# A causal convolution of 31 taps by 128 odd frequencies of 256 points with a transform of 60 points for its wrapped sums, and weight splits in another order around it

## Chip, core and metric

One core of a Trainium2 chip runs the whole kernel in one launch. The metric is the device time in microseconds (us); a run's time is that of one execution, and the profile is of one further execution on the same kind of chip.

## What is computed

One decoder layer for 256 tokens of width 1024, in float32: RMS norm, one input projection, eight heads of causal attention beside a convolution branch, an output projection over both with a residual, then a gated feed-forward network (width 2816) with a residual. The branch that the change is about, cut from the reference:

```
h = a * sigmoid(g)                      # (256 tokens, 512 channels)
h = pad(h, 30 tokens in front)          # causal
h = depthwise_conv(h, dw_w, 31 taps) + dw_b
h = silu(layer_norm(h over channels))   # becomes the lower half of the output projection's input
x = x + concat([attn, h]) @ w_out
```

## The kernel before

**Precision by splitting.** Every float32 operand of TensorE is split into a high part (a rounded copy, by ScalarE) and a low part (the difference, by VectorE), both of type float32r; a product is two or three matmuls (hi·hi, hi·lo, lo·hi). So each weight costs ScalarE one copy (`wh`, L196) and VectorE one subtraction (`wl`, L200) for every piece of 128 x 1024.

**Order of the work.** TensorE's program is written out by hand. Tasks (generators) are put between its groups of matmuls: `step()` runs what is due, `spawn` adds one. Every engine runs its instructions in the order in which they were written. Weights come in 47 blocks of 1 MB on SyncE's queue into four buffers. `feed(upto)` writes the copies `wh` up to piece upto+1 and the subtractions `wl` up to piece upto, and behind each odd `wl` the load of a block four further on. Seven piece buffers are in turn.

**The convolution.** It is done by frequencies, as matrix products with constant cosine and sine tables. `conv_task` makes `hf` (L230 and the two lines before it, by `mm3`): the transform over 288 points, which holds the 256 tokens and the 30 wrapped ones, has 145 frequencies. Real and imaginary parts of the first 128 fill two tiles of 128 rows (j = 0, 1), the 17 others with copies fill 68 rows of a third (j = 2). Each needs both token blocks of 128: 3 tiles x 2 blocks x 3 matmuls of 512 columns. VectorE multiplies by the taps' spectrum `Ws` (L546 to L548, L553) into `Y`; Y's rows are split into `yh`, `yl` (L181, L182). `ln_task` transforms back: two token blocks x 3 tiles x 3 matmuls into two PSUM banks `cv`; the third tile has a row of ones times `dw_b`, which adds the bias. Then come the statistics of the layer norm (`st`, `mv`, L578, L579), a reciprocal root by twelve small VectorE operations (L240 to L257) that ends in `nb` (L583), the normalised copy `yn` (L588, ScalarE), the transpose `cT` (L599, TensorE), Silu into `cs` (L602) and the split into `mix` (L181, L182).

**Around it.** The tile j = 2 is not made in the task: `third()` runs after the last group of the input projection (`p`, L624), between the two copies of the values `vs` (L631, L632, both ScalarE) and the attention's last products `O` (L644, L645). Behind `O` come the 18 matmuls of `cv`, and behind them the output projection in two halves of 8 groups of 12 matmuls `po` (L236): the first half takes the attention's rows of `w_out`, the second the convolution's. Each group ends in an addition on VectorE, `x2T` (L686), which frees the group's PSUM bank; there are four such banks in turn, shared with `p`, `O` and the feed-forward's `fg` and `fu`. In the second half, two ScalarE operations (`g` high L660, square `sq` L662), one on GpSimd (`acc`, L664) and one on VectorE (`g` low, L667) follow each `x2T`: they make the input of the feed-forward network and its sum of squares (`pss`, L698, then a root, `wide`, L703, and a transpose `prb`, L707).

In the input projection `feed` stops at piece 21. At each group of the output projection it is called with the piece of the group plus LEAD = 4, less one for the last two groups of the second half; a piece serves two groups. So the first group (piece 20) has the low parts of pieces 22, 23 and 24 written ahead of its `x2T`.

Of the kernel before, what the change touches and what calls it, by code (L numbers as in the profile page):

```python
# [9 lines left out]
F32R = mybir.dt.float32r  # L10
I32 = mybir.dt.int32
BF16 = mybir.dt.bfloat16
AF = mybir.ActivationFunctionType
ALU = mybir.AluOpType
AX = mybir.AxisListType

P = 128
D = 1024
T = 256
# [6 lines left out]
NF = FF // P  # L26
TAPS = 31
EPS = 1e-6
L = 288
NB = 47  # L30
BW = 2048
PIECE = 1024
R3 = 69
WARM = 18
RAW = 4
WGT = 7
# [31 lines left out]
def _parts(a):  # L68

    hi = _round12(a)  # L70
    return np.stack([hi, a - hi], 1)


def _constants():
    t = np.arange(T)[:, None]
    f = np.arange(L // 2 + 1)[None, :]
    ang = 2 * np.pi * ((t * f) % L) / L
    c, s = np.cos(ang), np.sin(ang)
    alpha = np.where((f == 0) | (f == L // 2), 1.0, 2.0) / L
    fwd = np.concatenate([c[:, :P], -s[:, :P], c[:, P:], -s[:, P:], c[:, P:], -s[:, P:]], 1)  # L80
    fwd = _parts(fwd.astype(np.float32).reshape(NT, P, 324).transpose(1, 0, 2))
    ir, ii = (alpha * c).T, (-alpha * s).T
    inv = np.zeros((3, P, T))
    inv[0], inv[1] = ir[:P], ii[:P]
    inv[2, :R3] = np.concatenate([ir[P:], -ir[P:], ii[P:], ii[P:], np.ones((1, T))], 0)
    inv = _parts(inv.astype(np.float32).transpose(1, 0, 2))
    lag = (TAPS - 1 - np.arange(TAPS))[:, None]
    ang = 2 * np.pi * ((lag * f) % L) / L
    c, s = np.cos(ang), np.sin(ang)
    fw = np.concatenate([c[:, :P], -s[:, :P], c[:, P:], -s[:, P:], -s[:, P:], c[:, P:]], 1)  # L90
    fw = fw.astype(np.float32)
    hi = _round12(fw)
    taps = np.zeros((96, 324), np.float32)
    taps[0:TAPS], taps[32:32 + TAPS], taps[64:64 + TAPS] = hi, hi, fw - hi
    out = {"fwd": fwd, "inv": inv, "taps": taps}
    freq = np.power(np.float32(10000.0), -np.arange(0, HD, 2, dtype=np.float32) / np.float32(HD)).astype(np.float32)
    ang = np.arange(T, dtype=np.float32)[:, None] * freq[None, :]
    cos, sin = np.cos(ang.astype(np.float64)), np.sin(ang.astype(np.float64))
    tab = np.concatenate([cos, cos, -sin, sin], 1).astype(np.float32)
    out["rope"] = np.ascontiguousarray(tab.reshape(NT, P, 2 * HD).transpose(1, 0, 2))  # L100
    q, k = np.arange(P)[:, None], np.arange(P)[None, :]
    tri = np.where(k <= q, 0.0, -1e30)
    out["mask"] = np.concatenate([tri, np.zeros((P, P)), tri], 1).astype(np.float32)
    out["ident"] = np.eye(P, dtype=np.float32)
    return out
# [20 lines left out]
def _build(nc, tc, t, ctx):  # L126
# [18 lines left out]
    def load(pl, name, shape, eng=nc.sync, **kw):  # L145
        tl = pl.tile(shape, F32, name="c_" + name, **kw)
        eng.dma_start(tl, t[name])
        return tl
# [78 lines left out]
    def mm3(out, lhs, rhs, start, stop):  # L227
        nc.tensor.matmul(out, lhs[0], rhs[0], start=start, stop=False)  # L228
        nc.tensor.matmul(out, lhs[0], rhs[1], start=False, stop=False)
        nc.tensor.matmul(out, lhs[1], rhs[0], start=False, stop=stop)  # L230
# [93 lines left out]
            load_block(4)  # L324
    ident = load(const, "ident", [P, P])
    load_block(5)
    taps = load(early, "taps", [96, 324], tag="Y", bufs=3)
    dwr = early.tile([96, W], F32, name="dwr", tag="Y", bufs=3)
    nc.sync.dma_start(dwr, t["dw_w"])
    mask = load(early, "mask", [P, 3 * P])  # L330

    G = {}
    spans = ((0, P), (P, P), (2 * P, R3 - 1))
    spl = (slice(0, P), slice(P, 3 * P))
    v = early.tile([P, NT + 2 * NT * H], F32, name="v")
    c = early.tile([P, NT + 2 * NT * H], F32, name="c")
# [26 lines left out]
        G["cols"] = load(const, "cols", [P, 16])  # L363

    def spectra_task():
        tapr = early.tile([96, 324], F32R, name="tapr")
        nc.scalar.activation(tapr, taps, AF.Copy)
        dws = early.tile([96, W], F32R, name="dws")
        nc.scalar.activation(dws, dwr, AF.Copy)
        nc.vector.tensor_tensor(dws[32:64, :], dwr[32:64, :], dws[32:64, :].bitcast(F32), op=ALU.subtract)  # L370
        yield PW_GAP
        Ws = G["Ws"] = early.tile([P, 3, W], F32, name="Ws")
        for j, (o, n) in enumerate(spans):
            b = t_bank(f"pw{j}")
            nc.tensor.matmul(b[:n, :], tapr[:, o:o + n], dws, start=True, stop=True)
            nc.scalar.activation(Ws[:n, j, :], b[:n, :], AF.Copy)
            yield 1
        Y = G["Y"] = [work(f"Y{j}", "Y", 3) for j in range(3)]
        nc.sync.dma_start(Y[2][R3 - 1:R3, :], t["dw_b"])

    def rope_half(bank, z, i, name):
        hw = HD // 2
# [47 lines left out]
    def q_task(banks):  # L430
        kqT = keep.tile([P, 2, 4, T], F32, name="kqT", tag="x2T")
        G["kT"], G["qT"] = kqT[:, 0], kqT[:, 1]
        qr, totals = [], []
        for i in range(NT):
            t1, total = rope_half(banks[i], 0, i, "q")
            totals.append(total)
            qr.append(t1)
            if i == 0:
                yield Q_GAP
        spawn(transposed(qr, G["qT"], "q"), QT_WAIT)  # L440
        yield 1
        for i in range(NT):
            r3 = heads3(G["kr"][i])
            nc.vector.tensor_tensor(r3, r3, cqk[1][:, i, :, None].to_broadcast([P, H, HD]), op=ALU.mult)
        spawn(transposed(G["kr"], G["kT"], "k"), KT_WAIT)
        yield 1
        for total in totals:
            total()
        mean_square(0)
        root(late_part)  # L450
        G["scq"] = early.tile([P, NT, H], F32, name="scq")
        nc.gpsimd.tensor_scalar(G["scq"], cqk[0], HD ** -0.5, None, op0=ALU.mult)
        for name, shape in (("fwd", [P, 2, NT, 324]), ("inv", [P, 2, 3, T])):
            tl = early.tile(shape, F32R, name=name)
            nc.gpsimd.dma_start(tl, t[name])
            G[name] = (tl[:, 0], tl[:, 1])
        yield S_WAIT
        G["sums"] = early.tile([P, NT, H], F32, name="sums")
        G["pT"] = [None] * H
        for j in range(H // 2):  # L460
            spawn(pair_task(j), 3 * j)
# [53 lines left out]
    def conv_task(banks):  # L515
# [15 lines left out]
        hf = []  # L531

        def spectrum(j):
            o, n = spans[j]
            b = t_bank(f"hf{j}", "s" if j < 2 else "t")
            for i in range(NT):
                mm3(b[:n, :], [f[:, i, o:o + n] for f in fwd], (hh[:, i, :], hl[:, i, :]), i == 0, i == NT - 1)
            hf.append(b)

        for j in range(2):  # L540
            spectrum(j)
            yield 1
        Ws, Y = G["Ws"], G["Y"]
        for j in range(2):
            pa, pb = (work(f"y{a}{j}", "tmp", 6) for a in "ab")
            nc.vector.tensor_tensor(pa, hf[0], Ws[:, j, :], op=ALU.mult)  # L546
            nc.vector.tensor_tensor(pb, hf[1], Ws[:, 1 - j, :], op=ALU.mult)
            nc.vector.tensor_tensor(Y[j], pa, pb, op=(ALU.subtract, ALU.add)[j])  # L548

        def third():  # L550

            spectrum(2)
            nc.vector.tensor_tensor(Y[2][:R3 - 1, :], hf[2][:R3 - 1, :], Ws[:R3 - 1, 2, :], op=ALU.mult)  # L553

        G["third"] = third
        while "vs" not in G:
            yield 1
        yh = early.tile([P, 3, W], F32R, name="yh", tag="hh")
        yl = early.tile([P, 3, W], F32R, name="yl", tag="hl")
        G["ys"] = [(yh[:n, j, :], yl[:n, j, :]) for j, n in enumerate((P, P, R3))]  # L560
        for j in range(3):
            n = P if j < 2 else R3
            split(G["ys"][j], Y[j][:n, :], nc.vector)

    def ln_task():
        inv = G["inv"]
        cv = []
        st = early.tile([P, NT, 6], F32, name="st")
        mv = early.tile([P, NT, 2], F32, name="mv")
        vv = early.tile([P, NT], F32, name="vv")  # L570
        for i in range(NT):
            b = t_bank(f"cv{i}", "s")
            for a, j in enumerate(range(3)):
                n = P if j < 2 else R3
                mm3(b, [m[:n, j, i * P:(i + 1) * P] for m in inv], G["ys"][j], a == 0, a == 2)
            cv.append(b)
        for i in range(NT):
            nc.vector.bn_stats(st[:, i, :], cv[i])  # L578
            nc.vector.bn_aggr(mv[:, i, :], st[:, i, :])  # L579
        nc.vector.tensor_scalar(vv, mv[:, :, 1], EPS, None, op0=ALU.add)  # L580
        lr = rsqrt(early, vv, NT, "lr")
        nb = early.tile([P, NT], F32, name="nb")
# [46 lines left out]

    vs = G["vs"] = early.tile([P, NT, W], F32, name="vs", tag="sg")  # L630
    nc.scalar.activation(vs[:, 0, :], banks[0], AF.Copy, scale=rstd1[:, 0:1])  # L631
    nc.scalar.activation(vs[:, 1, :], banks[1], AF.Copy, scale=rstd1[:, 1:2])  # L632
    G["third"]()
    mix = G["mix"] = [keep.tile([P, KT, T], F32R, name="mix" + s, tag="big_" + s) for s in "hl"]
    O = [None, None]
# [21 lines left out]
    def x2_task(d):  # L657
# [7 lines left out]
        if d < KT - 1:  # L665
            yield 1
        nc.vector.scalar_tensor_tensor(ffn["l"][:, d, :], x, g2[:, d:d + 1], ffn["h"][:, d, :].bitcast(F32),  # L667
                                       op0=ALU.mult, op1=ALU.subtract)

    for half in range(2):  # L670
        for d in range(KT):
            step()
            feed(off // PIECE + (LEAD if half == 0 or d < OUT_LATE else LEAD - 1))
            if half == 1 and d == 0:
                early_ctx.close()
                late = ffn["late"] = pool("late")
# [123 lines left out]
def _layout(a):  # L800
# [19 lines left out]
    for n in ("q_norm_g", "k_norm_g"):  # L820
# [10 lines left out]
        "gqk": rep(np.stack(gqk)),  # L831
        "dw_w": np.tile(np.concatenate([A["dw_w"][0], np.zeros((1, W), np.float32)], 0), (3, 1)),
        "dw_b": A["dw_b"],
    }


# [14 lines left out]
```

## Time and profile before

| | us |
|---|---|
| median of 3 runs (lowest, highest) | 298.63 (298.60, 298.77) |
| the profiled execution's own time | 299.09 |
| its span in the profile | 297.0 |
| TensorE busy in the span | 290.5 |
| VectorE, ScalarE, GpSimd busy | 222.1, 173.5, 22.2 |

PE is TensorE's matmuls, PEld its weight loads, DVE VectorE, ACT ScalarE, POOL GpSimd, SP the engine whose queue issues most DMAs. A matmul's recorded duration is longer than its spacing from the next, since matmuls are pipelined: 128 x 512 ones follow each other every 0.23 us, 128 x 256 ones every 0.12 us. On DVE too an operation that does not need the result of the one ahead starts a little before that one's recorded end. Times in the views count from the start of the span. All TensorE work of this execution ran at the full granted clock.

### The profile page before, as it was taken

The page shows a single profiled execution, that of the slowest core. Times are in us where ns is not written, and L with a number is a line of the kernel's source. Part 1 is how long each engine was busy: PE and PEld are TensorE (multiplying, and loading weights), DVE is VectorE, ACT ScalarE, POOL GpSimd, SP SyncE. Part 2 cuts the span into 40 slices and gives each one's busy share as a digit, 9 for nine tenths or more (in the row PEclk, how much of TensorE's full clock was granted, in tenths as well). Part 3 has the DMA queues.
Part 4 walks back from the last instruction along what each step waited for, and adds up shares of the span by engine and source line. Part 5 has one row for each costly group of instructions (what it writes and reads, how often), then busy time and mean ns, then how long its engine had stood idle before and what let it go on. Part 6 is the DMA issues. An engine that isn't in the chain of part 4 may idle for free.

```text
span 297.0 us, 4413 instructions
## 1 busy us (share of the span) xinstructions
PE 290.5 (98%) x1663; PEld 250.1 (84%) x1663; DVE 222.1 (75%) x413; ACT 173.5 (58%) x304; POOL 22.2 (7%) x41
## 2 busy tenths in 40 slices
PE   8999999999989999999999999999999999999994
PEld 6888877677789998888888888888888888888884
DVE  3899986999688999788888887787787666455412
ACT  5776759877846684566666665755755544344000
POOL 0005381000000270000000000000000000000000
PEclk9999999999999999999999999999999999999999
DMA  7999768434207527356464654655644636530000
GB/s 258 413 412 374 291 267 319 172 141 164 121 0 285 177 108 282 141 168 259 148 257 164 221 205 157 231 180 154 238 175 151 231 121 249 185 127 18 18 20 18
DMA packets 10759, 56.59 MB, mean 191 GB/s; under 512 B 1457, under 2 KB 3089, under 8 KB 4850
## 3 DMA queue, kind: packets, MB, share of 16 engines
q1 hardware_dynamic: 10306, 54.86, 50.5%
q0 software_dynamic: 288, 1.45, 1.4%
q8 instruction: 13, 0.21, 0.3%
q14 instruction: 8, 0.07, 0.1%
q10 hardware_dynamic: 144, 0.00, 0.0%
HBM read 55.26 MB, written 1.05 MB: 190 GB/s over the span
## 4 chain that ended last, share of the span: by engine, by line
PE 96%; DVE 2%; issue 1%
PE p L624 19%; PE fg L215 14%; PE fu L215 14%; PE pd L215 12%; PE fu L220 7%; PE fg L220 7%; PE pd L220 6%; PE po L236 6%; PE pd L786 2%; PE warm L281 1%; PE S L469 1%; PE pT L499 1%; PE pdl L795 1%; PE O L644 1%; PE cv L228 1%
## 5 line engine op out<-in xcount | busy, mean ns | idle before, releaser
L200 DVE TENSOR_TENSOR wl<-raw,wh 128x1024 fp32r<-128x1024 f32 x90 | 109.3, 1231 | 0.0
L196 ACT ACTIVATE wh<-raw 128x1024 fp32r<-128x1024 f32 x90 | 92.6, 1048 | 6.2 <-PE pd L215 3.3
L215 PE MATMUL fg<-g,wh 128*128 128x512 f32 x176 | 44.5, 393 | 0.0
L215 PE MATMUL fu<-g,wh 128*128 128x512 f32 x176 | 44.5, 393 | 0.0
L215 PE MATMUL pd<-act,wh 128*128 128x512 f32 x154 | 38.9, 392 | 0.0
L215 PEld LDWEIGHTS fu<-g,wh 128*128 128x128 f32 x176 | 31.7, 189 | 5.7
L215 PEld LDWEIGHTS fg<-g,wh 128*128 128x128 f32 x176 | 31.6, 189 | 5.6
L624 PE MATMUL p<-wh,xh 128*128 128x512 f32 x80 | 33.0, 413 | 0.0
L215 PEld LDWEIGHTS pd<-act,wh 128*128 128x128 f32 x154 | 27.6, 189 | 4.8
L624 PE MATMUL p<-wh,xl 128*128 128x512 f32 x80 | 31.5, 394 | 0.0
L220 PEld LDWEIGHTS fg<-g,wl 128*128 128x128 f32 x176 | 24.1, 190 | 1.8
L220 PEld LDWEIGHTS fu<-g,wl 128*128 128x128 f32 x176 | 24.1, 190 | 1.7
L624 PE MATMUL p<-wl,xh 128*128 128x512 f32 x80 | 25.1, 393 | 0.0
L225 DVE TENSOR_TENSOR o<-pd,os 128x256 f32<-128x256 f32 x8 | 3.4, 424 | 28.8 <-ACT os L224 28.8
L220 PE MATMUL fu<-g,wl 128*128 128x256 f32 x176 | 24.8, 282 | 0.0
L220 PE MATMUL fg<-g,wl 128*128 128x256 f32 x176 | 24.8, 282 | 0.0
L224 ACT ACTIVATE os<-pd 128x256 f32<-128x256 f32 x8 | 3.1, 384 | 35.3 <-PE pd L220 30.7
L716 ACT ACTIVATE sf<-tg 128x256 f32<-128x256 f32 x22 | 9.2, 419 | 23.6 <-DVE tg L714 23.6
L220 PEld LDWEIGHTS pd<-act,wl 128*128 128x128 f32 x154 | 21.2, 190 | 1.7
L220 PE MATMUL pd<-act,wl 128*128 128x256 f32 x154 | 21.7, 282 | 0.0
L721 ACT ACTIVATE act<-ac 128x256 fp32r<-128x256 f32 x22 | 9.2, 418 | 21.0 <-DVE ac L720 21.0
L225 DVE TENSOR_TENSOR ac<-fu,us 128x256 f32<-128x256 f32 x22 | 9.3, 424 | 14.1 <-ACT us L224 14.1
(157 smaller groups left out, 405.6 us busy)
## 6 DMA issues: line engine op xcount, KB each, us to landing
raw<-w SPq DMA_DIRECT2D x45, 1024.0 KB, 4.8
first<-first SPq DMA_DIRECT2D x8, 384.0 KB, 6.3
xtok<-xtok SPq DMA_DIRECT2D x2, 512.0 KB, 9.1
x2T<-xT SPq DMA_DIRECT2D x1, 1024.0 KB, 8.3
out<-o SPq DMA_DIRECT2D x8, 128.0 KB, 1.7
inv<-inv POOLq DMA_DIRECT2D x1, 768.0 KB, 6.9
fwd<-fwd POOLq DMA_DIRECT2D x1, 648.0 KB, 4.1
c_glub<-glub SPq DMA_DIRECT2D x1, 512.0 KB, 9.3
```

Source lines behind the costliest of these rows:

```text
L196: nc.scalar.activation(dst[0], src, AF.Copy)
L200: nc.vector.tensor_tensor(dst[1], src, dst[0].bitcast(F32), op=ALU.subtract)
L215: nc.tensor.matmul(out.rearrange("p (a q) -> p a q", a=2), w[0], both, start=z in first and z not in seen, stop=False)
L220: nc.tensor.matmul(out[:, 0:T], w[1], both[:, 0, :], start=False, stop=z in last and left[z] == 0)
L224: nc.scalar.activation(side, bank[:, T:], AF.Copy)
L225: nc.vector.tensor_tensor(out, bank[:, 0:T], side, op=ALU.add)
L228: nc.tensor.matmul(out, lhs[0], rhs[0], start=start, stop=False)
L236: nc.tensor.matmul(out, l, r, start=a == 0, stop=a == len(ops) - 1)
L624: nc.tensor.matmul(banks[i], (xh, xh, xl)[a][:, kt, sls[i]], w[a % 2], start=kt == 0 and a == 0, stop=kt == KT - 1 and a == 2 - (order[-1] ...
L716: nc.scalar.activation(s, tg, AF.Silu)
L721: nc.scalar.activation(acts[:, 0, f, :], ac, AF.Copy)
L786: nc.tensor.matmul(both, w[0], act, start=f == 0, stop=f == NF - 1)
```

## The change

The convolution is done modulo another polynomial: 128 odd frequencies of 256 points, whose real and imaginary parts fill two tiles of 128 rows exactly. The sums that wrap round come back at the first 30 tokens with the other sign; a transform of 60 points (30 odd frequencies, 4 x 30 = 120 rows) over the last 30 tokens, which lie in token block 1, makes the correction, and it is added to token block 0 alone. So:

- `hf` j = 2 has 120 rows instead of 68 and one token block instead of two (3 matmuls instead of 6).
- `cv` runs block 1 first, without the third tile (6 matmuls), then block 0 with it (9). Block 1 gets its bias by an addition on VectorE from a copy of `dw_b` on all partitions (`cvb`, in SBUF), which a new DMA of 256 KB on SyncE's queue loads behind the load of `dw_b`.
- The second `vs` copy is VectorE's (`tensor_scalar`) instead of ScalarE's, and the last step of Y[1] is written behind it, in `third()`.
- `feed(22)` is written between the statistics of block 1 and those of block 0; in the output projection's first half `feed` leads by 2 for six groups, then by 3, in the second half by 3, then 4, then 3.
- The constant tables change size: fwd from 2 x 648 to 2 x 632 columns, inv from 2 x 768 to 2 x 640, taps from 324 to 376.

```diff
-spans = ((0, P), (P, P), (2 * P, R3 - 1))
+spans = ((0, P), (P, P), (2 * P, TAIL))          # TAIL = 4 * 30
 ...
 (spectra_task)
-        nc.sync.dma_start(Y[2][R3 - 1:R3, :], t["dw_b"])
+        nc.sync.dma_start(Y[2][TAIL:TAIL + 1, :], t["dw_b"])
+        G["bias"] = load(early, "dw_bb", [P, W])
 ...
 (conv_task)
-            for i in range(NT):
-                mm3(b[:n, :], [f[:, i, o:o + n] for f in fwd], (hh[:, i, :], hl[:, i, :]), i == 0, i == NT - 1)
+            for i in range(NT) if j < 2 else (1,):
+                o = i * T + j * P if j < 2 else 2 * T
+                mm3(b[:n, :], [f[:, o:o + n] for f in fwd], (hh[:, i, :], hl[:, i, :]), i == 0 or j == 2, i == NT - 1)
 ...
-        for j in range(2):
+        def combine(j):
             pa, pb = (work(f"y{a}{j}", "tmp", 6) for a in "ab")
             nc.vector.tensor_tensor(pa, hf[0], Ws[:, j, :], op=ALU.mult)
             nc.vector.tensor_tensor(pb, hf[1], Ws[:, 1 - j, :], op=ALU.mult)
-            nc.vector.tensor_tensor(Y[j], pa, pb, op=(ALU.subtract, ALU.add)[j])
+            return lambda: nc.vector.tensor_tensor(Y[j], pa, pb, op=(ALU.subtract, ALU.add)[j])
+        combine(0)()
+        second = combine(1)
         def third():
+            second()
             spectrum(2)
 ...
 (ln_task)
-        for i in range(NT):
+        for i in (1, 0):
             b = t_bank(f"cv{i}", "s")
-            for a, j in enumerate(range(3)):
-                n = P if j < 2 else R3
-                mm3(b, [m[:n, j, i * P:(i + 1) * P] for m in inv], G["ys"][j], a == 0, a == 2)
-            cv.append(b)
-        for i in range(NT):
+            for j in range(2):
+                o = j * T + i * P
+                mm3(b, [m[:, o:o + P] for m in inv], G["ys"][j], j == 0, i == 1 and j == 1)
+            if i == 0:
+                mm3(b, [m[:TAIL + 1, 2 * T:] for m in inv], G["ys"][2], False, True)
+                cv[i] = b
+            else:
+                cv[i] = work("cvb", "tmp", 6)
+                nc.vector.tensor_tensor(cv[i], b, G["bias"], op=ALU.add)
             nc.vector.bn_stats(st[:, i, :], cv[i])
             nc.vector.bn_aggr(mv[:, i, :], st[:, i, :])
+            if i:
+                feed(V_PIECE + 1)
 ...
-    nc.scalar.activation(vs[:, 1, :], banks[1], AF.Copy, scale=rstd1[:, 1:2])
+    nc.vector.tensor_scalar(vs[:, 1, :], banks[1], rstd1[:, 1:2], None, op0=ALU.mult)
 ...
+    def lead(half, d):
+        if half:
+            return LEAD if 0 < d < OUT_LATE else LEAD - 1
+        return LEAD - 2 + (d >= OUT_LATE)
 ...
-            feed(off // PIECE + (LEAD if half == 0 or d < OUT_LATE else LEAD - 1))
+            feed(off // PIECE + lead(half, d))
```

## Rows read from the trace of the kernel before

**Rows 1.** The page's first part (busy time of each engine, share of the span) and its chain that ended last, shares by engine.

```profile
PE 290.5 (98%) x1663; PEld 250.1 (84%) x1663; DVE 222.1 (75%) x413; ACT 173.5 (58%) x304; POOL 22.2 (7%) x41
...
PE 96%; DVE 2%; issue 1%
```

**Rows 2.** Busy time by stretch. Columns: stretch, its length, busy us (instructions) of PE, PEld, DVE, ACT, POOL, granted TensorE clock, DMA share, GB/s. The first stretch is the first groups of the output projection, the second its second half, the last most of the feed-forward network.

```profile
82.40:89.70 7.30, 5.94 (x50) 5.74 (x48) 6.66 (x19) 2.56 (x4) 0.00 (x0) 1.00 0.07 11
...
96.30:107.90 11.60, 11.60 (x99) 11.60 (x99) 10.94 (x19) 8.21 (x17) 5.09 (x5) 1.00 0.54 182
...
125.00:231.00 106.00, 106.00 (x609) 93.26 (x609) 85.19 (x139) 66.92 (x119) 0.00 (x0) 1.00 0.54 192
```

**Rows 3.** Waits from 60 to 125 us: engine, what waited <- for what, us in total, times, longest.

```profile
DVE mixl L182 <- ACT mixh L181: 1.5, 3, 0.9
...
PE po L236 <- DVE x2T L686: 1.4, 1, 1.4
...
PEld O L644 <- ACT vs L632: 0.4, 1, 0.4
```

**Rows 4.** The timeline from 73.3 to 79 us, all engines: start, duration, engine, line, operation, what it writes <- reads, shapes, count, idle time before it and what ended that.

```profile
73.34 0.62 PE L624 MATMUL p<-wl,xh 128*128 128x512 f32 x2
...
73.79 0.39 PE L228 MATMUL hf<-hh,fwd 128*68 128x512 f32 x1
...
74.95 0.39 PE L230 MATMUL hf<-hh,fwd 128*68 128x512 f32 x1
75.27 0.20 PEld L644 LDWEIGHTS O<-pTs,vs 128*64 128x64 f32 x4 [0.41 <-ACT vs L632]
...
75.37 0.69 DVE L553 TENSOR_TENSOR Y<-hf,Ws 68x512 f32<-68x512 f32 x1 [1.20 <-PE hf L230]
75.42 1.67 ACT L181 ACTIVATE yh<-Y 128x512 fp32r<-128x512 f32 x3 [0.39 <-ACT vs L632]
...
76.08 1.89 DVE L182 TENSOR_TENSOR yl<-Y,yh 128x512 fp32r<-128x512 f32 x3
...
78.07 0.50 PE L228 MATMUL cv<-yh,inv 128*128 128x512 f32 x1
```

**Rows 5.** Groups of instructions over the span, shapes kept apart: busy us, mean ns of one, idle before.

```profile
L632 ACT ACTIVATE vs<-p,c 128x512 f32<-128x512 f32 x1 | 0.7, 679 | 0.0
...
L546 DVE TENSOR_TENSOR ya<-hf,Ws 128x512 f32<-128x512 f32 x2 | 1.4, 684 | 0.0
...
L508 DVE SCALAR_TENSOR_TENSOR ug<-p,c,c_glub 128x512 f32<-128x512 f32 x2 | 1.4, 738 | 0.0
```

**Rows 6.** The timeline from 82 to 91.2 us, columns as in rows 4.

```profile
82.39 0.28 PE L236 MATMUL po<-mixh,wh 128*128 128x256 f32 x1
...
82.59 0.70 DVE L578 BATCH_NORM_STATS2 st<-cv 128x6 f32<-128x512 f32 x1 [1.19 <-PE cv L230]
...
85.78 3.49 DVE L200 TENSOR_TENSOR wl<-raw,wh 128x1024 fp32r<-128x1024 f32 x3
...
89.19 0.75 DVE L686 TENSOR_TENSOR x2T<-po,x2T 128x256 f32<-128x256 f32 x2
...
89.67 0.39 PE L236 MATMUL po<-mixh,wh 128*128 128x256 f32 x1 [1.36 <-DVE x2T L686]
...
91.19 1.04 PE L599 MATMUL cT<-c_ident,yn 128*128 128x128 f32 x8
```

**Rows 7.** DVE's timeline from 95 to 110 us.

```profile
95.16 0.69 DVE L182 TENSOR_TENSOR mixl<-cs,mixh 128x512 fp32r<-128x512 f32 x1 [0.88 <-ACT mixh L181]
95.77 0.42 DVE L686 TENSOR_TENSOR x2T<-po,x2T 128x256 f32<-128x256 f32 x1
96.11 1.22 DVE L200 TENSOR_TENSOR wl<-raw,wh 128x1024 fp32r<-128x1024 f32 x1
97.24 0.75 DVE L686 TENSOR_TENSOR x2T<-po,x2T 128x256 f32<-128x256 f32 x2
...
103.23 1.76 DVE L200 TENSOR_TENSOR wl<-raw,wh 128x1024 fp32r<-128x1024 f32 x1
...
107.00 0.49 DVE L667 SCALAR_TENSOR_TENSOR g<-x2T,c_cols,g 128x256 fp32r<-128x256 f32 x1
108.09 0.42 DVE L686 TENSOR_TENSOR x2T<-po,x2T 128x256 f32<-128x256 f32 x1 [0.60 <-PE po L236]
```

**Rows 8.** PE's timeline at the head of the feed-forward network.

```profile
107.89 1.55 PE L215 MATMUL fg<-g,wh 128*128 128x512 f32 x6
...
112.07 0.50 PE L698 MATMUL pss<-one,acc 128*128 128x1 f32 x4
...
116.70 0.38 PE L707 MATMUL prb<-c_ident,wide 128*128 128x128 f32 x2
```

**Rows 9.** POOL's timeline from 95 to 128 us, then one line of DVE's from 106 to 140 us.

```profile
103.03 2.56 POOL L664 TENSOR_TENSOR acc<-acc,sq 128x256 f32<-128x256 f32 x2 [0.73 <-ACT sq L662]
...
109.52 1.81 POOL L664 TENSOR_TENSOR acc<-acc,sq 128x256 f32<-128x256 f32 x1 [0.61 <-ACT sq L662]
...
115.62 0.29 DVE L703 COPY wide<-rstd 128x256 f32<-128x256 f32 x1
```

**Rows 10.** DMA issues: out <- in, queue, count, KB each, median us from issue to landing; then a line of SP's timeline.

```profile
c_glub<-glub SPq DMA_DIRECT2D x1, 512.0 KB, 9.3
...
40.97 0.33 SPq L379 DMA_DIRECT2D Y<-dw_b  x1
```

More of the change, by code (lines that the diff above doesn't have):

```diff
@@ L28 @@
 EPS = 1e-6
-L = 288
+LAGS = TAPS - 1
 NB = 47
@@ L32 @@
 PIECE = 1024
-R3 = 69
+TAIL = 4 * LAGS
 WARM = 18
@@ L74, in _constants, with waves @@
 def _constants():
[L75 to L91, printed above, removed]
+    def waves(n, t):
+        ang = 2 * np.pi * ((t[:, None] * (2 * np.arange(n // 2) + 1)[None, :]) % (2 * n)) / (2 * n)
+        return np.cos(ang), -np.sin(ang)
+    c, s = waves(T, np.arange(T))
+    ct, st = waves(2 * LAGS, np.arange(P) - (P - LAGS))
+    fwd = np.concatenate([c[:P], s[:P], c[P:], s[P:], np.where(np.arange(P)[:, None] < P - LAGS, 0.0,
+                                                              np.concatenate([ct, st, ct, st], 1))], 1)
+    fwd = _parts(fwd.astype(np.float32))
+    ir, ii = waves(2 * LAGS, np.arange(P) + LAGS)
+    tail = np.concatenate([ir, -ir, ii, ii], 1).T / LAGS * (np.arange(P) < LAGS)
+    tail = np.concatenate([tail, np.ones((1, P)), np.zeros((P - TAIL - 1, P))], 0)
+    inv = _parts(np.concatenate([c.T * 2 / T, s.T * 2 / T, tail], 1).astype(np.float32))
+    lag = TAPS - 1 - np.arange(TAPS)
+    c, s = waves(T, lag)
+    ct, st = waves(2 * LAGS, lag)
+    fw = np.concatenate([c, s, ct, st, st, ct], 1).astype(np.float32)
     hi = _round12(fw)
-    taps = np.zeros((96, 324), np.float32)
+    taps = np.zeros((96, 2 * P + TAIL), np.float32)
     taps[0:TAPS], taps[32:32 + TAPS], taps[64:64 + TAPS] = hi, hi, fw - hi
@@ L326, in _build @@
     load_block(5)
-    taps = load(early, "taps", [96, 324], tag="Y", bufs=3)
+    taps = load(early, "taps", [96, 2 * P + TAIL], tag="Y", bufs=3)
     dwr = early.tile([96, W], F32, name="dwr", tag="Y", bufs=3)
@@ L365, in spectra_task @@
     def spectra_task():
-        tapr = early.tile([96, 324], F32R, name="tapr")
+        tapr = early.tile([96, 2 * P + TAIL], F32R, name="tapr")
         nc.scalar.activation(tapr, taps, AF.Copy)
@@ L452, in q_task @@
         nc.gpsimd.tensor_scalar(G["scq"], cqk[0], HD ** -0.5, None, op0=ALU.mult)
-        for name, shape in (("fwd", [P, 2, NT, 324]), ("inv", [P, 2, 3, T])):
+        for name, shape in (("fwd", [P, 2, 2 * T + TAIL]), ("inv", [P, 2, 2 * T + P])):
             tl = early.tile(shape, F32R, name=name)
@@ L533, in spectrum @@
         def spectrum(j):
-            o, n = spans[j]
+            n = spans[j][1]
             b = t_bank(f"hf{j}", "s" if j < 2 else "t")
-            for i in range(NT):
-                mm3(b[:n, :], [f[:, i, o:o + n] for f in fwd], (hh[:, i, :], hl[:, i, :]), i == 0, i == NT - 1)
+            for i in range(NT) if j < 2 else (1,):
+                o = i * T + j * P if j < 2 else 2 * T
+                mm3(b[:n, :], [f[:, o:o + n] for f in fwd], (hh[:, i, :], hl[:, i, :]), i == 0 or j == 2, i == NT - 1)
             hf.append(b)
@@ L547, in conv_task @@
             nc.vector.tensor_tensor(pb, hf[1], Ws[:, 1 - j, :], op=ALU.mult)
-            nc.vector.tensor_tensor(Y[j], pa, pb, op=(ALU.subtract, ALU.add)[j])
+            return lambda: nc.vector.tensor_tensor(Y[j], pa, pb, op=(ALU.subtract, ALU.add)[j])
+        combine(0)()
+        second = combine(1)
         def third():
+            second()
             spectrum(2)
-            nc.vector.tensor_tensor(Y[2][:R3 - 1, :], hf[2][:R3 - 1, :], Ws[:R3 - 1, 2, :], op=ALU.mult)
+            nc.vector.tensor_tensor(Y[2][:TAIL, :], hf[2][:TAIL, :], Ws[:TAIL, 2, :], op=ALU.mult)
         G["third"] = third
@@ L559, in conv_task @@
         yl = early.tile([P, 3, W], F32R, name="yl", tag="hl")
-        G["ys"] = [(yh[:n, j, :], yl[:n, j, :]) for j, n in enumerate((P, P, R3))]
+        G["ys"] = [(yh[:n, j, :], yl[:n, j, :]) for j, n in enumerate((P, P, TAIL + 1))]
         for j in range(3):
-            n = P if j < 2 else R3
+            n = P if j < 2 else TAIL + 1
             split(G["ys"][j], Y[j][:n, :], nc.vector)
@@ L566, in ln_task @@
         inv = G["inv"]
-        cv = []
+        cv = [None, None]
         st = early.tile([P, NT, 6], F32, name="st")
@@ L570, in ln_task @@
         vv = early.tile([P, NT], F32, name="vv")
-        for i in range(NT):
+        for i in (1, 0):
             b = t_bank(f"cv{i}", "s")
-            for a, j in enumerate(range(3)):
-                n = P if j < 2 else R3
-                mm3(b, [m[:n, j, i * P:(i + 1) * P] for m in inv], G["ys"][j], a == 0, a == 2)
-            cv.append(b)
-        for i in range(NT):
+            for j in range(2):
[7 more added lines that the diff above has]
+                nc.vector.tensor_tensor(cv[i], b, G["bias"], op=ALU.add)
             nc.vector.bn_stats(st[:, i, :], cv[i])
             nc.vector.bn_aggr(mv[:, i, :], st[:, i, :])
+            if i:
+                feed(V_PIECE + 1)
         nc.vector.tensor_scalar(vv, mv[:, :, 1], EPS, None, op0=ALU.add)
@@ L833, in _layout @@
         "dw_b": A["dw_b"],
+        "dw_bb": rep(A["dw_b"][0]),
     }
```

## The prediction

> **What bounds the kernel now.** I read the page's busy shares first, then the chain that ended last, then busy time by stretch, then the waits and the timeline of the stretch that the change touches. TensorE is busy for 290.5 of 297.0 us and is 96% of the chain [rows 1]: the end moves by TensorE's own work and its holes, and by other engines' work only where TensorE waits for them. From 125 to 231 us it has no hole at all, at the full clock [rows 2], so what is won or lost before about 117 us arrives at the end unchanged. The part that the change touches has one large hole: from 82.4 to 89.7 us PE works for 5.94 of 7.30 us [rows 2], and the waits put the missing 1.4 us down to VectorE's `x2T` [rows 3]. The timeline shows why: the fifth `po` group needs the bank that the first `x2T` frees; that addition starts at 89.19, behind three weight splits from 85.78 on, behind the layer norm's root that starts with `st` at 82.59 [rows 6]. The second thing to see is DVE in the output projection's second half: 10.94 us of 11.60 [rows 2]. It has nearly nothing to spare there, so work that is put into that stretch can come out at the other end.
>
> **The change, part by part.** The sum is made against the profiled execution's 299.09 us; the median of the runs is 298.63, lower by 0.46, and I take the same difference off at the end. Until 73.3 us I expect no change: the new DMA of 256 KB is issued behind `dw_b` at 40.97 us; a load of twice its size took 9.3 us to land [rows 10], and its data is first read near 79 us. The smaller tables save a little transfer that nothing waits for.
>
> *Third spectrum.* Six matmuls from 73.79 to the last one's start at 74.95, 0.23 us each [rows 4], become three: 0.69 us less of PE. 120 rows instead of 68 make the weight load longer, which lies under the matmul ahead. What follows on PE is `O`, which now starts at 75.27, released by the second `vs` [rows 4]; the matmuls themselves held PE until 75.18 (74.95 + 0.23), so that wait cost only 0.1. After the change the three matmuls leave PE at 74.5 (73.79 + 3 x 0.23), and `O` waits for `vs` on DVE. DVE was idle for 1.20 us ahead of `Y` at 75.37 [rows 4], so it takes this over at once: start at 74.0, just after the last `p` matmul's end at 73.96 (73.34 + 0.62) [rows 4], duration 0.68 to 0.74, by a one-PSUM-source product and by a longer form with the same scalar operand [rows 5]; I take 0.7, near the product's. It ends at 74.7, and with 0.1 us to PE `O` starts at 74.8: 0.47 us won. Bounds: all 0.69 if the hand-over costs nothing, nothing at all if it costs half a microsecond.
>
> ScalarE's copy of `vs` took 0.679 us and a VectorE operation of the same size on PSUM 0.684 [rows 5], so the engine is no dearer in this trace. [...]
>
> *Moved Y steps.* Y[1]'s last step now lies behind `vs` on DVE. At a spacing of 0.6 us (1.89 us for the three `yl` [rows 4]) DVE does `vs` 74.0, Y[1] 74.6, Y[2] 75.2, `yl` from 75.8, where it was 76.08 [rows 4]. `yh` was held until the last `hf` matmul, 75.42 [rows 4], since it takes the buffer of `hh`; now it can start at 74.75. So `cv` has its operands in time, and the moved step costs nothing as long as DVE's 1.20 us of idle time covers it; without that it would cost 0.6.
>
> *Inverse transform.* `O` lasts from 75.27 to 78.07 [rows 4], so it ends at 77.6. `cv` takes 4.32 us from 78.07 to the first `po` at 82.39 [rows 4, 6] for 18 matmuls, and 15 take 3 x 0.234 less, 3.62. The first `po` starts at 81.2: 0.47 + 0.70 = 1.17 us earlier.
>
> *Added bias, earlier split.* Block 1's bank is ready at 77.6 + 6 x 0.234 + 0.2 = 79.2. DVE then does `cvb` 0.70, `st` 0.70, `mv` 0.2 and the split of piece 22 (1.14, from 3 in 3.41 us between 85.78 and 89.19 [rows 6]) and is free at 82.0, where block 0 has been ready since 81.4. So `cvb` is hidden under block 0's nine matmuls, the split is not quite, and `st` of block 0 still starts 0.6 us earlier than the 82.59 of before. If nothing covered it, `cvb` would cost its 0.7. From this `st` to `nb`'s end is 3.19 us (82.59 to 85.78 [rows 6]), and with no split ahead of it the first `x2T` starts at 85.2, not 89.19.
>
> *The hole.* PE reaches the fifth group 4 x 12 x 0.12 = 5.76 us after the first `po`, at 87.0; its bank is free at 85.6. Before, it would have come at 88.15 and came at 89.67 [rows 6]: 1.52 us won, the whole hole. Sum up to here: 0.47 + 0.70 + 1.52 = 2.69. `cT` moves from 91.19 [rows 6] to 88.5; the second half starts that much earlier too.
>
> *The price: splits put off.* A lead of 2 puts pieces 25 and 26 behind `cT`'s products, where before only 27 and later were left. DVE stands still before that, waiting for `mixh` (1.5 us in three waits [rows 3]), so the time cannot be made up. `mixl` at 95.16 hangs on `cT` and moves to 92.5. From there to the end of the sixth `g` low took 12.33 us (95.16 to 107.49 [rows 7]); now two splits more, 2 x 1.14, less some 0.25 us of idle time that fills up: 14.35, so 106.8. PE starts `fg` at 107.89 - 2.69 = 105.2 [rows 8] and wants that `g`, the sixth of its series, 5 x 0.23 later, at 106.35. So it waits 0.5 us. On the way, `x2T` of the seventh group ends at 92.5 + 0.6 + 0.34 + 2 x 1.14 + 0.42 = 96.1 against PE's need at 96.4: 0.3 us to spare. Piece 26, the tightest, is split by 95.7 and used from 99.3.
>
> *Behind it.* Where DVE waited 0.60 us for PE before the last `x2T` [rows 7], it now comes straight on, at 106.65: 1.44 us earlier than before, while PE is 2.2 earlier. `pss` had 0.74 us to spare behind GpSimd's last `acc` (109.52 + 1.81 against 112.07 [rows 8, 9]) and `prb` 0.8 behind `wide` (115.62 + 0.29 against 116.70 [rows 8, 9]). Both slacks are just used up, so nothing is added, or 0.1. SyncE's queue: the block that follows piece 23 is asked for at about the same time, the one behind piece 25 some 3.5 us later, near 94.7; it is copied near 107, so the load (9.3 us at the worst seen [rows 10]) still lies under other work.
>
> *Sum:* 0.47 + 0.70 + 1.52 - 0.5 = 2.2 us; 299.09 - 2.2 = 296.9 beside the profile, 298.63 - 2.2 = **296.4** by the median.
>
> **Rivals.**
> *DVE keeps up.* If the moved splits cost less or fill more idle time, PE does not wait for the sixth `g`: 2.69 to 2.9 us won, 295.8. For it: the wait is the difference of two long sums. Against it: the splits' spacing of 1.14 is well known [rows 6]. Chance 0.18.
>
> *The hole moves.* The 0.3 us to spare at the seventh `x2T` are little. If DVE comes out of `mixl` a microsecond later (ScalarE's copies stand ahead of `cs`), PE stands at that bank and later at `g` for 1.5 us in all instead of 0.5: 1.2 won, 297.4. Chance 0.17. With DVE later by 1.7 to 2.5, nothing measurable is left, 298.5; chance 0.10.
>
> *DVE against GpSimd.* One split took 1.76 us instead of 1.22, at 103.23, while GpSimd was adding from 103.03 on [rows 7, 9]. Put off, more splits can meet these additions, which began only with the second half's squares. If three of them are each held for a whole addition of 1.1 us (the row's two took 2.56 with their gaps [rows 9]), DVE is later by 3 x 1.1 - 0.54 = 2.8 and the result is 0.6 slower, 299.2. This decides once DVE loses more than 2.2. Against it: only two splits, of pieces 29 and 30, lie behind the second square, and the one before met an addition already. Chance 0.05. [...]
>
> **How the numbers follow.** The forecast has 0.50. The range takes in the rivals but the last two: 295.7 (the third spectrum's 0.69 won whole, no wait at `g`) to 297.9 (0.7 us won). About 0.2%, 0.6 us, is what a measurement of this kernel tells from none. Faster by more: 0.50 + 0.18 + 0.17 = 0.85, less 0.01 for what I have not seen; within it 0.10; slower 0.06.
>
> **What would show it.** Right: 3 matmuls of `hf` with 120 rows, 15 of `cv`; no wait of `po` for `x2T`; `O` near 74.8, first `po` near 81.2, `cT` near 88.5; `fg` near 105.2, and inside its first group a wait of about 0.5 us for `g` low. Wrong: `vs` on DVE above 0.8 us or `O` behind 75.2; `st` of block 0 behind 82.6; a wait for `x2T` at the seventh or a later group; splits of 1.7 us and more in the second half; or PE waiting for `pss` or `prb` by more than 0.3 us.

## The result, and the profile after

The changed kernel takes 296.76 us (median of 4 runs, 296.71 to 297.18) against 298.63: a ratio of 0.9934 with a 95% interval from 0.9921 to 0.9946, or 1.9 us. A second series beside other kernels gave 297.12 against 298.88, 1.8 us.

The profiled execution took 296.76 us, 2.33 us less than the one before (299.09), and its span is 294.6. Some 0.45 us of that is not the change's. The third spectrum's first matmul starts at 73.34 where it was 73.79 [rows 4], with nothing altered ahead of it but a DMA and table sizes; the section on the hardware shows where such differences arise. So times are compared from that matmul on. From it to `prb`, behind which TensorE has no hole in either kernel until the last groups, it was 42.91 us (116.70 - 73.79 [rows 4, 8]) and is 41.00 (114.34 - 73.34): **1.91 us**, as the medians say.

First the page: busy times, and the shares of the chain that ended last.

```profile
PE 289.1 (98%) x1657; PEld 248.8 (84%) x1657; DVE 223.3 (76%) x415; ACT 172.6 (59%) x303; POOL 21.1 (7%) x41
...
PE 89%; DVE 7%; ACT 2%; issue 2%; DVEq 0%
```

Six matmuls are gone and DVE has two operations more. TensorE's share of the chain fell from 96% [rows 1] to 89%: a piece of the path now runs over DVE. Busy time by stretch (columns as in rows 2) says which. The stretches are the same times as before, and the program is by then up to 2.8 us further on:

```profile
82.40:89.70 7.30, 7.30 (x64) 7.30 (x63) 5.89 (x19) 3.51 (x6) 0.00 (x0) 1.00 0.26 103
96.30:107.90 11.60, 11.28 (x83) 10.45 (x82) 11.54 (x21) 9.66 (x20) 6.13 (x7) 1.00 0.64 253
125.00:231.00 106.00, 106.00 (x610) 93.27 (x609) 85.04 (x140) 66.34 (x120) 0.00 (x0) 1.00 0.54 199
```

The hole of the first stretch is closed. In the second, DVE is busy for all but 0.06 us, and TensorE, which was full there [rows 2], stands idle for 0.3. The waits between 60 and 125 us name what it waits for:

```profile
DVE mixl L184 <- ACT mixh L183: 2.5, 2, 1.6
...
PEld fg L217 <- DVE g L681: 0.7, 1, 0.7
...
PEld O L658 <- ACT vs L645: 0.4, 1, 0.4
PEld prb L727 <- DVE wide L723: 0.3, 1, 0.3
PE fg L217 <- DVE g L681: 0.3, 1, 0.3
```

The wait for `x2T` [rows 3] is gone; a wait for the sixth `g` low and one for `wide` are new. The timeline from 73 to 88 us, all engines, answers to rows 4 and 6:

```profile
73.30 0.69 ACT L645 ACTIVATE vs<-p,c 128x512 f32<-128x512 f32 x1 [0.67 <-PE p L638]
73.34 0.39 PE L230 MATMUL hf<-hh,fwd 128*120 128x512 f32 x1
73.54 0.75 DVE L646 TENSOR_SCALAR vs<-p,c 128x512 f32<-128x512 f32 x1 [0.59 <-PE p L638]
...
74.13 0.65 PE L658 MATMUL O<-pTs,vs 128*64 128x256 f32 x3
...
77.09 0.50 PE L230 MATMUL cv<-yh,inv 128*128 128x512 f32 x1
...
80.70 0.28 PE L238 MATMUL po<-mixh,wh 128*128 128x256 f32 x1
...
81.46 0.69 DVE L590 BATCH_NORM_STATS2 st<-cv 128x6 f32<-128x512 f32 x1
...
84.65 0.76 DVE L706 TENSOR_TENSOR x2T<-po,x2T 128x256 f32<-128x256 f32 x2
...
87.90 1.04 PE L613 MATMUL cT<-c_ident,yn 128*128 128x128 f32 x8
```

And DVE from 90 to 108 us, PE at the head of the feed-forward network, POOL, and DVE's `wide` (rows 7, 8, 9):

```profile
90.31 0.69 DVE L184 TENSOR_TENSOR mixl<-cs,mixh 128x512 fp32r<-128x512 f32 x1 [1.64 <-ACT mixh L183]
...
92.82 2.35 DVE L202 TENSOR_TENSOR wl<-raw,wh 128x1024 fp32r<-128x1024 f32 x2
...
101.95 1.76 DVE L202 TENSOR_TENSOR wl<-raw,wh 128x1024 fp32r<-128x1024 f32 x1
...
105.57 0.63 DVE L681 SCALAR_TENSOR_TENSOR g<-x2T,c_cols,g 128x256 fp32r<-128x256 f32 x1
106.12 0.41 DVE L706 TENSOR_TENSOR x2T<-po,x2T 128x256 f32<-128x256 f32 x1
106.46 1.50 DVE L681 SCALAR_TENSOR_TENSOR g<-x2T,c_cols,g 128x256 fp32r<-128x256 f32 x2
107.89 4.03 DVE L202 TENSOR_TENSOR wl<-raw,wh 128x1024 fp32r<-128x1024 f32 x3
```

```profile
104.61 1.33 PE L217 MATMUL fg<-g,wh 128*128 128x512 f32 x5
106.26 0.50 PE L217 MATMUL fg<-g,wh 128*128 128x512 f32 x1 [0.32 <-DVE g L681]
...
109.41 0.50 PE L718 MATMUL pss<-one,acc 128*128 128x1 f32 x4
...
114.34 0.44 PE L727 MATMUL prb<-c_ident,wide 128*128 128x128 f32 x2
```

```profile
105.04 3.52 POOL L678 TENSOR_TENSOR acc<-acc,sq 128x256 f32<-128x256 f32 x4 [0.73 <-ACT sq L676]
...
113.99 0.29 DVE L723 COPY wide<-rstd 128x256 f32<-128x256 f32 x1
```

The group of six `fg` matmuls [rows 8] is now five and one: the sixth comes 1.65 us after the first, not 5 x 0.23. That is how a wait inside a group shows when PE's idle column gives only the part behind the modelled end of the matmul ahead.

### The profile page after: what moved, and what is told of

Read it like the earlier page. It is cut to its first block, busy times and chain, and to the rows that moved or that the text cites. A ratio compares the mean times of both kernels' runs of the same rounds, so it can differ in the third digit from the quotient of the medians.

```text
span 294.6 us, 4405 instructions
## 1 busy us (share of the span) xinstructions
PE 289.1 (98%) x1657; PEld 248.8 (84%) x1657; DVE 223.3 (76%) x415; ACT 172.6 (59%) x303; POOL 21.1 (7%) x41
## 4 chain that ended last, share of the span: by engine, by line
PE 89%; DVE 7%; ACT 2%; issue 2%; DVEq 0%
PE p L638 19%; PE fu L217 13%; PE fg L217 12%; PE pd L217 12%; PE fu L222 7%; PE fg L222 6%; PE pd L222 6%; DVE wl L202 3%; PE po L238 2%; PE pd L806 2%; PE warm L283 1%; DVE x2T L706 1%; PE S L472 1%; PE pT L502 1%; DVE g L681 1%
```

## The experiments

"To prb" is the time from the third spectrum's first matmul to the start of `prb`, of the run's profile. Each ratio is to the kernel before in the runs on the same chip, whose medians were 298.63 us for the change, 298.81 for conv_alone, order_alone, lead3_from_fifth and vs_scalar, 298.88 for the change again, third_twice, no_bias_add and no_acc, and 299.09 for lead3_again and order_lead3.

| kernel | median us | ratio (95%) | to prb | against before |
|---|---|---|---|---|
| before | 298.63 | | 42.91 | |
| the change | 296.76 | 0.9934 (0.9921 to 0.9946) | 41.00 | -1.91 |
| the change again | 297.12 | 0.9943 (0.9928 to 0.9957) | 41.01 | -1.90 |
| conv_alone | 297.65 | 0.9950 (0.9931 to 0.9968) | 41.69 | -1.22 |
| order_alone | 298.28 | 0.9976 (0.9964 to 0.9988) | 42.22 | -0.69 |
| vs_scalar | 297.32 | 0.9940 (0.9921 to 0.9959) | 41.26 | -1.65 |
| third_twice | 297.69 | 0.9958 (0.9943 to 0.9972) | 41.52 | -1.39 |
| no_bias_add | 297.19 | 0.9945 (0.9930 to 0.9960) | 40.99 | -1.92 |
| no_acc | 295.78 | 0.9893 (0.9876 to 0.9909) | 40.06 | -2.85 |
| lead3_from_fifth | 296.19 | 0.9901 (0.9877 to 0.9926) | 40.06 | -2.85 |
| lead3_again | 296.03 | 0.9904 (0.9885 to 0.9923) | 40.07 | -2.84 |
| order_lead3 | 297.59 | 0.9949 (0.9932 to 0.9966) | 41.29 | -1.62 |

**The two halves of the change.** The new convolution with the old order of the splits:

```diff
-            if i:
-                feed(V_PIECE + 1)
 ...
-            feed(off // PIECE + lead(half, d))
+            feed(off // PIECE + (LEAD if half == 0 or d < OUT_LATE else LEAD - 1))
```

> The new convolution with the old places of the weight splits (lead of 4, no split between the two statistics). Times against 298.63 before and 296.76 with the whole change. Theory (matmuls and order are two separate gains, and the order also costs): TensorE's six matmuls and the earlier O give 1.2 us at the first po; x2T again stands behind three splits, so the fifth po group waits 1.3 to 1.5 us for it; no wait at the sixth g low or at prb, since no split was put off. 1.2 us faster than before, 297.4. Rival A (the matmuls are the whole gain, the order only moves waits): 296.8 as with the whole change. Rival B (the order is the whole gain, the matmuls are swallowed by the wait for x2T): 298.6.

And the old convolution with the new order (the `feed(V_PIECE + 1)` behind the statistics of the first block, and `lead`):

> The old convolution with the new places of the weight splits (a lead of 2, 3, 4, 3 and one split between the two statistics). Theory: the wait of the fifth po group (1.4 to 1.5 us) goes; the two splits that now lie behind mixl make the sixth g low late by 0.5 us for TensorE and wide by 0.3 for prb; 0.7 us faster, 297.9. Rival A: nothing, 298.6. Rival B: 296.8, as with the whole change.

Both came out as the theory had it, by 1.22 and 0.69 us, and 1.22 + 0.69 is the whole 1.91: neither half swallows the other. Rivals A and B both fall. The waits of the first from 60 to 125 us, then those of the second:

```profile
PEld po L238 <- DVE x2T L704: 1.6, 1, 1.6
PE po L238 <- DVE x2T L704: 1.4, 1, 1.4
```

```profile
PEld fg L215 <- DVE g L669: 0.7, 1, 0.7
...
PEld prb L715 <- DVE wide L711: 0.3, 1, 0.3
```

The hole belongs to the old order and the waits for `g` and `wide` to the new one, whichever convolution runs.

**The price of the splits put off.** One number of the change altered:

```diff
-            return LEAD - 2 + (d >= OUT_LATE)
+            return LEAD - 2 + (d >= 4)
```

> The whole change with one number altered: the lead rises from 2 to 3 at the fifth group of the first half, not the seventh. So the split of piece 25 is written in front of the two mixl, into VectorE's 1.64 us of waiting ahead of them, and not behind. Theory (VectorE's lateness behind mixl is what still holds TensorE back): the waits for the sixth g low (0.7 on the weight load) and for prb (0.3) go, 0.75 us faster than the whole change, 296.0. Rival A (those waits cost TensorE nothing, or come back at another place at once): 296.8. Rival B (the two earlier copies on ScalarE delay cs and with it mixl): slower than the change, 297.2 or more.

> The whole change with the lead of 3 from the fifth group on, once more with more rounds, beside the next one. All theories, by the run before: 2.5 to 2.8 us faster than the kernel before, 296.1 to 296.4; no wait for g low or prb. From the third spectrum's first matmul to prb 40.06 us, where the kernel before has 42.91.

> The old convolution with the new order and the lead of 3 from the fifth group on. Theory (the put-off split is the whole price of the new order; without it the order is worth the full hole of the fifth group, whatever the convolution): no wait for x2T, none for the sixth g low or prb, 1.5 us faster than before, 297.3; from the third spectrum to prb 41.4 us. Rival (the old convolution's later cT leaves VectorE late all the same): the waits stay, 0.6 us faster as with the lead of 2, 298.2.

The split of piece 25 moves from behind the two `mixl` to ahead of them. DVE's timeline of the first run:

```profile
87.74 2.35 DVE L202 TENSOR_TENSOR wl<-raw,wh 128x1024 fp32r<-128x1024 f32 x2
90.01 0.42 DVE L706 TENSOR_TENSOR x2T<-po,x2T 128x256 f32<-128x256 f32 x1
90.92 0.69 DVE L184 TENSOR_TENSOR mixl<-cs,mixh 128x512 fp32r<-128x512 f32 x1 [0.49 <-ACT mixh L183]
```

DVE's wait ahead of the first `mixl` shrinks from 1.64 to 0.49 us: the split fills it. Of TensorE's waits from `O` on only these are left:

```profile
PEld O L658 <- ACT vs L645: 0.4, 1, 0.4
PEld cv L230 <- issue: 0.2, 1, 0.2
```

`prb` comes 0.94 us sooner than with the change, more than the 0.75 expected. With the old convolution the order so mended is worth 1.62, and 1.22 + 1.62 is the 2.84 of both. So one split in the wrong place cost the change 0.94 us, a third of what it could have won. This version is the fastest of those that do the whole computation: 296.03 us, with 299.09 for the kernel before in the same series.

**GpSimd's part in DVE's lateness.** The seven additions left out:

```diff
-        if d:
-            nc.gpsimd.tensor_tensor(ffn["acc"], ffn["acc"], sq, op=ALU.add)
```

> The whole change without GpSimd's seven additions into acc, so that the sum of squares holds the first eighth alone. Theory (GpSimd's additions lengthen VectorE's work in the second half): the split that took 1.76 us takes 1.22 and the pairs of g low 1.0 to 1.15 instead of 1.50; VectorE comes to the sixth g low 0.7 to 0.9 us earlier and to wide 1.2 us earlier, the waits for both (0.7 on the weight load, 0.3) go: 0.6 to 0.8 us faster than the whole change, 296.1. Rival (the two put-off splits alone make the waits, GpSimd has no part): split and g low last as before, 296.8.

```profile
102.83 1.22 DVE L202 TENSOR_TENSOR wl<-raw,wh 128x1024 fp32r<-128x1024 f32 x1
...
106.48 0.47 DVE L679 SCALAR_TENSOR_TENSOR g<-x2T,c_cols,g 128x256 fp32r<-128x256 f32 x1
107.14 0.48 DVE L679 SCALAR_TENSOR_TENSOR g<-x2T,c_cols,g 128x256 fp32r<-128x256 f32 x1 [0.18 <-ACT g L674]
```

The split of 1.76 us takes 1.22, and every `g` low 0.47 to 0.48. Both waits go, and the path to `prb` is as short as with the split moved, 40.06: this is TensorE's own work. That is 0.94 us by the profile, where 0.6 to 0.8 was expected, and `wide` comes 1.95 us sooner, not 1.2. So lateness has two parents, the put-off split and GpSimd's additions, and taking either away is enough. The rival, that GpSimd has no part, falls.

How much an operation lost went with the addition that was under way when it started. In the change's run:

```profile
101.74 0.88 POOL L678 TENSOR_TENSOR acc<-acc,sq 128x256 f32<-128x256 f32 x1 [0.73 <-ACT sq L676]
...
106.88 0.80 POOL L678 TENSOR_TENSOR acc<-acc,sq 128x256 f32<-128x256 f32 x1
...
107.11 0.85 DVE L681 SCALAR_TENSOR_TENSOR g<-x2T,c_cols,g 128x256 fp32r<-128x256 f32 x1
```

The split at 101.95 starts with 0.67 us of the addition left (101.74 + 0.88 - 101.95) and takes 0.54 longer than in no_acc. The last `g` low, at 107.11, starts with 0.57 left and takes 0.38 longer; the one at 105.57 starts with 0.35 left and takes 0.16 longer. Each of the three lost what was left of the addition, less 0.13 to 0.19 us. What the two engines contend for, no run shows.

**The single terms.** Three runs price parts of the sum.

```diff
-    nc.vector.tensor_scalar(vs[:, 1, :], banks[1], rstd1[:, 1:2], None, op0=ALU.mult)
+    nc.scalar.activation(vs[:, 1, :], banks[1], AF.Copy, scale=rstd1[:, 1:2])
```

> The whole change, but the second vs copy back on ScalarE. Theory (O waits for ScalarE's last vs copy, as it did before): ScalarE's second copy would end 0.6 us behind the first, so O, cv and everything behind them start 0.6 us later: 297.4. Rival (O needs the first copy alone and the second is in time on either engine): 296.8.

Between the two: 0.26 us later than the change by the profile. The medians put it at 0.2 to 0.6 against the change's two series, but the intervals of the ratios overlap, so the profile alone shows it. The theory falls in its first half: `O`'s first weight load did not wait for the second copy; it came 0.79 us after the third spectrum's first matmul with either engine. The second product did wait:

```profile
74.37 0.19 PEld L658 LDWEIGHTS O<-pTs,vs 128*64 128x64 f32 x2 [0.38 <-ACT vs L645]
...
74.86 0.13 PEld L659 LDWEIGHTS O<-pTs,vs 128*64 128x64 f32 x1 [0.30 <-ACT vs L646]
```

```diff
-            for i in range(NT) if j < 2 else (1,):
+            for i in range(NT) if j < 2 else (1, 1):
```

> The whole change with the third spectrum's three matmuls written twice, the second group starting its bank anew, so six matmuls as before the change. Theory (what the three saved matmuls are worth is their 0.69 us less the 0.1 that O waits for vs anyhow): O, cv, po, cT 0.6 us later, and everything behind: 297.4. Rival (VectorE's vs and Y steps hold O and cv, the matmuls are covered): 296.8.

0.52 us by the profile, 0.57 by the medians: the three matmuls are on the path, and `O` is back at 1.49 us after the first, as before (1.48). The rival falls. Here both copies of `vs` end well ahead of `O` (by 74.67, an estimate: DVE's copy ended 0.95 us after the third spectrum's first matmul in the change, and that matmul is at 73.72; `O` is at 75.21, and the waits put none of its time down to a copy), and `O` lasts 2.80 us (to `cv` at 78.01), as before.

```diff
-                cv[i] = work("cvb", "tmp", 6)
-                nc.vector.tensor_tensor(cv[i], b, G["bias"], op=ALU.add)
+                cv[i] = b
```

> The whole change without cvb: block 1's statistics and normalised copy read the PSUM bank, so the bias of the second 128 tokens is left out. Theory (the added 0.7 us of VectorE lies under block 0's nine matmuls, and what is left comes back before x2T is due): st of block 0 up to 0.6 us earlier, first x2T too, TensorE's times as with the whole change: 296.8, within 0.15. Rival (the added operation costs what it lasts): 0.7 us faster than the whole change, 296.1.

Counted from the third spectrum, block 0's `st` comes 0.56 us earlier (81.28 - 73.72 against 81.46 - 73.34), the first `x2T` too, and TensorE's times do not move by more than 0.01: the added operation is hidden. Its lines on DVE:

```profile
81.28 0.70 DVE L589 BATCH_NORM_STATS2 st<-cv 128x6 f32<-128x512 f32 x1
...
84.48 0.76 DVE L705 TENSOR_TENSOR x2T<-po,x2T 128x256 f32<-128x256 f32 x2
```

> The whole change once more, beside the three others on the same chip. All theories: 1.9 us faster than before, with the waits for the sixth g low (0.7 on the weight load) and for prb (0.3).

That run agreed with the first: 0.7 us of waiting for the sixth `g` low, 0.4 for `wide` where the first had 0.3, and 41.01 to `prb`.

## Why the prediction was right

The direction, the mechanism and nearly the size held: 2.2 us foretold, 1.9 measured. By its steps, with times from the third spectrum's first matmul (73.79 before, 73.34 after):

- **Third spectrum and `O`:** 0.69 us won (`O` at 1.48, now 0.79), the upper bound; 0.47 was taken. The weight loads of 120 columns took 0.18 us where those of 68 took 0.14, under the matmuls ahead, which still follow each other every 0.23. The step had `O` wait for DVE's copy. Its first product needs ScalarE's copy alone, and the 0.1 us that the step put down to a wait for `vs` is there without one (1.49 in third_twice). The second copy then holds the second product: it ends 0.16 us behind the start of `O` in the change (73.54 + 0.75 against 74.13), 0.44 in vs_scalar (74.13 + 0.68 against 74.37) and ahead of it in third_twice, and `O` lasts 2.96, 3.24 and 2.80 us. So part is given back: `cv` comes 0.53 earlier, against 0.47 foretold. That these two are so close is luck: a wait that was not there and a hold that was not seen nearly cancel. DVE was the dearer engine for the copy, 0.75 us against ScalarE's 0.69, where the prediction called it no dearer by a row of 0.684; the sum was off for another reason.
- **Inverse transform:** the first `po` 1.24 us earlier, 1.17 foretold.
- **Bias and early split:** `st` and the first `x2T` at 81.9 and 85.1 on the clock of before, 82.0 and 85.2 foretold; hidden, as no_bias_add shows.
- **The hole:** closed whole; `cT` is 2.84 us earlier, 2.69 foretold.
- **Splits put off:** the sixth `fg` matmul 0.50 us late, just the 0.5 of the step, and the seventh `x2T` in time. Its cause is shown by lead3_from_fifth and order_alone.
- **Behind it:** this is the term that was mis-sized. The step let `pss` and `prb` come level with their operands and added nothing, or 0.1. By `pss` the gain is 2.21, 0.13 less than the 2.84 - 0.50 that was left: the matmul behind the one that had waited follows it 0.33 us later (106.26 to 106.59), not 0.23. `pss` itself had 0.85 us to spare behind GpSimd's last addition (105.04 + 3.52 against 109.41), so that slack was not used up. `prb` waited 0.30 more. For it the step carried the 1.42 us from the last `x2T` to the next split over from the kernel before:

```profile
108.44 1.15 DVE L667 SCALAR_TENSOR_TENSOR g<-x2T,c_cols,g 128x256 fp32r<-128x256 f32 x2
109.51 4.03 DVE L200 TENSOR_TENSOR wl<-raw,wh 128x1024 fp32r<-128x1024 f32 x3
```

But with DVE running without its 0.60 us pause [rows 7], the last two `g` low meet GpSimd's unbroken row of four additions (3.52 us), take 1.50 us as a pair instead of 1.15, and the next split starts 1.77 us behind that `x2T` (107.89 - 106.12). no_acc takes GpSimd away, and that wait with it.

So 2.84 - 0.50 - 0.13 - 0.30 = 1.91. The total is closer than its terms: ahead of `fg` the gain was 0.15 larger than foretold (2.84 against 2.69), which hides a third of the 0.43 that was missed behind it. Of the rivals, "DVE keeps up" is what lead3_from_fifth is. "DVE against GpSimd" named a real cause, but what it added to DVE's time over the kernel before is 0.35 us (1.77 - 1.42), not 2.8.

## What to carry to other kernels

When a change closes a hole, look next at the engine whose work was moved to close it: put that work into a wait that this engine has anyway (here 1.64 us ahead of `mixl`), not behind it. Do not count on durations carried over from a stretch with pauses once it has none (here 1.42 us became 1.77), least of all where another engine's work lengthens its own (here 1.22 us to 1.76). And write down for every released instruction which of its operands it waits for, tile by tile: a copy on another engine may hold the second product only (here for 0.30 us in vs_scalar).

## What was not expected of the hardware

Runs differ at their very start. In the same unaltered code the first matmuls of the input projection follow each other more slowly than the 0.23 us that they settle at: after 0.59, 0.43, 0.43 and 0.33 us before (up to 6.78 us in the span), after 0.59, 0.43, 0.42 and 0.43 in lead3_from_fifth (up to 6.90), after 0.43, 0.29 and 0.33 in the change's run (up to 6.08). The granted clock is given as 1.00 there in the profiles before and of the change (5 to 10 us) and of no_acc (5 to 7 us), so the cause stays open. In no_acc PE also stands idle for 0.28 us ahead of the matmul at 8.77 us, which waits for a weight copy. The third spectrum started between 73.31 and 74.40 us over the twelve profiles, a spread of more than half of the effect, with at most table sizes and one DMA altered ahead of it. The consequence is to compare such small effects from a fixed instruction on.
